# A hybrid decoder layer in fp32 on one core: the last stage's residual rows turned by VectorE, a norm of the first way down by VectorE, three placings

## The chip, the cores and the metric

The kernel runs on one core of one Trainium2 chip. The metric is the device time of one execution in microseconds (us), the median over runs. TensorE is called PE below, its weight loads PEld, VectorE DVE, ScalarE ACT, GpSimd POOL and SyncE SP.

## The reference, cut to what matters

One decoder layer over a sequence of 1024 tokens of width 1024, all in float32:

```
f = swiglu(rmsnorm(h, ffn1_pre_g), ffn1_w_gu, ffn1_w_down);  h = h + 0.5 * rmsnorm(f, ffn1_post_g)
m = hybrid_mixer(rmsnorm(h, mix_pre_g), ...)                  ;  h = h + rmsnorm(m, mix_post_g)
c = memory_cross_attention(rmsnorm(h, xa_pre_g), ...)         ;  h = h + rmsnorm(c, xa_post_g)
f = swiglu(rmsnorm(h, ffn2_pre_g), ffn2_w_gu, ffn2_w_down);  out = h + 0.5 * rmsnorm(f, ffn2_post_g)
swiglu(h) = (silu(g) * u) @ w_down, with g, u the halves of h @ w_gu;  rmsnorm(x, g) = x * rsqrt(mean(x*x) + eps) * g
```

The hidden width of the two feed-forward blocks is 2816. The mixer runs a stick-breaking attention of 16 heads beside a state-space scan (SSD), joins both and multiplies by `w_out`.

## The kernel before, in words

**Precision and tiles.** A float32 number is kept as a high and a low part (`xh`/`xl`, `whi`/`wlo`); a product is three matmuls on PE (`mm3`), each 128x128 by 128x512. ACT makes a high part (CAST, L268, or ACTIVATE, L275), DVE the low part by subtraction (L270, L277). Activations lie with channels on the partitions, in two halves of 512 tokens (half 0 and half 1); the last stage alone has its output with tokens on the partitions.

**Order.** PE's instructions are chained in the order in which the program writes them. A clock of modelled PE time runs along; side work is put on a list with a due time (`self.later`, `at`) and is written when the clock gets there. A scheduler then orders every other engine's instructions, with a priority for what stands in `urgent()`; an engine runs its instructions in the order in which they then stand. `lead` in `turned` is the modelled time by which a norm's matmul is put behind.

**The ways down** (`down7`) multiply by `w_down` with seven block products m = 0 to 6 instead of eight. Each m has eleven pairs of blocks (a weights' block and an activations' block, each split), twelve matmuls a pair, in steps of `sizes` = 2, 1, ..., 2 pairs; m = 6 has 2, 1, 1, 1, 1, 1, 4. In a step, i = 0 to 3 runs over the four banks of PSUM. The last four m's gather in banks `dn`, four buffers, so m + 1 writes the bank that m has left once DVE has added it to `F` (L1141). In the last stage (`down_rows`), bank 3 of m = 6 starts as a copy of `F[1][7]` (ACT, COPY dn<-F, L1152), because `on` is set for i = 3: its matmuls add to the copy. `F[1][7]` is final for that when m = 5's bank 3 has been added and the difference with `F[1][6]` is made. SP loads the blocks to come (`fetch`) into `raw` and `wraw`, two buffers each; for m = 6 DVE adds two blocks of weights into `wc` (L1119) ahead of the split. The activations' split is `hl`.

**The residual of the last stage.** The stored residual `h` has channels on the partitions, the last stage needs tokens there. For half 0, POOL's queue fetches each 128x512 row block by four DMAs of 32x16x32 (`fetch_rows`), and DVE turns it (`turn`, STREAM_TRANSPOSE). For half 1, POOL's queue fetches eight plain 128x512 tiles (`fetch_h`) and PE turns them by eight transposes for each block of 128 tokens (`shift`), between the last matmuls of m = 6; `end` adds the result, read from PSUM, into `F`, and `store` sends it out.

**The first way down** (`down1`) ends with `post(1, ...)`: the norm of the product (`cols`) by four matmuls `ms<-small,bh` into a column and four matmuls `ms<-ident,cpost` into rows, then `apply` (gain, residual) and `low` for each of eight tiles.

**The attention** prepares half of `w_out` beside its own work (`prepare`): load, split, store to DRAM (`dwhi`, `dwlo`), sixteen steps at due times. At its end the output product's operands are split by `mix_split(k)`: k = 0 to 4 by `before(n)` of the last head, 5 to 7 by the product's first two steps.

Of the kernel before, what the change touches and what calls it, by code (L numbers as in the profile page):

```python
# [10 lines left out]
F32 = mybir.dt.float32  # L11
F32R = mybir.dt.float32r
BF16 = mybir.dt.bfloat16
AF = mybir.ActivationFunctionType
ALU = mybir.AluOpType
# [32 lines left out]
class Kern:  # L48
# [296 lines left out]

    def turned(self, accs, ms, wait, c=None, out=None):

        nc, n = self.nc, accs[0].shape[1] // 32
        ps = self.t(self.msp, [P, H], F32, "ms", bufs=1)
        roots = []  # L350
        chains = self.floating is None
        for i, acc in enumerate(accs):
            self.turns += out is None
            part = self.part[self.turns % 2][:, 0:n]
            roots.append(self.roots[self.turns % 4] if out is None else out)
            self.kp(nc.vector.transpose(acc, acc))
            self.kp(
                nc.vector.tensor_reduce(
                    out=part, in_=acc.rearrange("p (j k) -> p j k", k=32), op=ALU.add, axis=mybir.AxisListType.X
                )  # L360
            )
            pin = self.pinned(self.clock + wait) if chains else nullcontext()
            with pin:
                self.mm(ps[:, 16 * i : 16 * i + n], self.one, part, True, True)
        for i, x in enumerate(roots):
            self.kp(nc.scalar.activation(x, ps[:, 16 * i : 16 * i + n], AF.Sqrt, bias=self.eps, scale=ms))
            self.kp(nc.vector.reciprocal(x, x))
        if c is not None:
            for q in range(4):
                k = slice(32 * q, 32 * q + 32)  # L370
                nc.gpsimd.tensor_copy(c[k], roots[0][k].rearrange("p (b q) -> p q b", q=4)[:, q])
        return roots
# [51 lines left out]
    def post(self, hh, gname, r2, gnext=None, out=None, step=None, spread=True, pins=(23000, 28000), accs=None, at=None, tail=None, hold=False, late=None, turn=(False, False), lead=2500):  # L424
# [13 lines left out]
        def cols():  # L438
            if turn[0]:
                roots.extend(self.turned(accs, 1.0 / D_MODEL, lead))  # L440
            else:
                self.rms_cols([accs], c, r2=r2)
# [597 lines left out]
    def down1(self, sp, wdn, act_d, xs_d, gpost, gnext):  # L1040
# [5 lines left out]
        accs = []  # L1046

        def squares(hh, d, tag):
            if d == 0:
# [6 lines left out]
        def finish(m, i):  # L1056
# [5 lines left out]
            elif m == 4:  # L1062
# [4 lines left out]
                self.post(0, gpost, self.C[0], gnext, step=2600, accs=accs[:], tail=(20500, 24000), late=38000, turn=(False, True))  # L1067
            elif m == 5:
                for d in range(4):
                    at(17000 + 2500 * d, squares, 1, d, "bh")  # L1070
# [6 lines left out]
        self.XH[1] = [self.t(self.xp, [P, H], F32R, f"xh1{d}") for d in range(KT)]  # L1077
        self.post(1, gpost, self.C[1], gnext, step=2000, accs=accs[:], at=(6500, 9000, 10000), tail=(7500, 11500), turn=(False, True))

    def down7(self, sp, wdn, act_d, xs_d, place, stay, finish, rows=True):  # L1080

# [60 lines left out]
        for m in range(7):  # L1142
# [13 lines left out]
            for n, size in enumerate(sizes):  # L1156
                ops = take(size)
                for i in range(4):
                    c = slice(i * P, i * P + P)
# [41 lines left out]
    def down_rows(self, sp, wdn, act_d, xs_d, out):  # L1201
# [15 lines left out]

        def fetch_h(d):
            self.kp(nc.gpsimd.dma_start(out=hs[1][d], in_=self.h[1][d]))

        def shift(tb):

            xt = [self.t(self.mmp, [P, H], F32, "mm") for _ in range(2)]
            for d in range(KT):
                self.tr(xt[d // 4][:, (d % 4) * P : (d % 4 + 1) * P], hs[1][d][:, tb * P : (tb + 1) * P])
            return xt

        def fetch_rows(tb, dh, behind):
# [8 lines left out]

        def turn(tb, dh):
            x = hs[0][2 * tb + dh]
            self.kp(nc.vector.transpose(x, x))  # L1240
# [41 lines left out]
        def finish(m, tb):  # L1282
# [11 lines left out]
            elif m == 4:  # L1294
                for tb in range(4):
# [4 lines left out]
                    at(11000 + 12000 * tb, early, tb)  # L1300
                for d in range(KT):
                    at(1000 + 2500 * d, fetch_h, d)
            elif m == 5:
# [14 lines left out]
        def last(tb):  # L1318
            xt = shift(tb)
            for dh in range(2):  # L1320
                end(1, tb, dh, xt)
                store(1, tb, dh, nc.sync)

        self.down7(sp, wdn, act_d, xs_d, place, stay, finish)


# [396 lines left out]
    def attention(self):  # L1723
        nc, ap = self.nc, self.ap
        with self.pools("at", ["o", "a"], ["w"]) as (op, sp, wsp, pp):
            self.prepare([("out", i) for i in range(8, 16)], *self.prep_pool(wsp), [self.clock + 30000 + 20000 * i for i in range(16)])
            turn = [0]
# [142 lines left out]
            def before(n):  # L1870

                for k in range(2 * n, 2 * n + 2) if n < 4 else ():
                    nc.gpsimd.dma_start(out=self.XL[0][k].bitcast(F32), in_=self.mix_d[8 + k][:, 0:H])
                if n > 7:
                    mix_split(n - 8)
                if n == 5:
# [156 lines left out]
            def beside():  # L2033
                mix_row(1)
                self.first = self.mix_first(ready.pop())
                for n in range(4 * MIXED):
                    if n < 2:
                        for k in ((5, 6), (7,))[n]:
                            mix_split(k)
                    if 4 <= n < 11:  # L2040
# [159 lines left out]
    def xattn(self):  # L2200
# [3 lines left out]
        with self.pools("xf", ["a", "b", "w"], []) as (sp, sp2, wsp, pp):  # L2204
# [107 lines left out]
            for s in range(8):  # L2312
# [3 lines left out]
                if s == 4:  # L2316
# [5 lines left out]
                    self.run_later(float("inf"))  # L2322
                    self.post(0, "xa_post_g", None, "ffn2_pre_g", step=5000, at=(5000, 11500, 14500), turn=(True, True))
                if s == 3:
# [245 lines left out]
```

## Time and profile before

| | |
|---|---|
| time, median of 3 runs | 2563.22 us (2559.22 to 2572.07) |
| the profiled execution's own time | 2560.25 us |
| its span on the chip | 2558.5 us |
| PE busy | 2539.2 us, 99% of the span |
| DVE, ACT, POOL busy | 2029.9, 1291.2, 600.2 us |
| instructions | 36552 |

Busy is the time in which an engine works on an instruction; the page gives it for each engine. A timeline row gives the start of a run of like instructions, their time together, and in brackets how long the engine had been idle before it and what released it.

### The profile page before, as it was taken

The page shows a single profiled execution, that of the slowest core. Times are in us where ns is not written, and L with a number is a line of the kernel's source. Part 1 is how long each engine was busy: PE and PEld are TensorE (multiplying, and loading weights), DVE is VectorE, ACT ScalarE, POOL GpSimd, SP SyncE. Part 2 cuts the span into 40 slices and gives each one's busy share as a digit, 9 for nine tenths or more (in the row PEclk, how much of TensorE's full clock was granted, in tenths as well). Part 3 has the DMA queues.
Part 4 walks back from the last instruction along what each step waited for, and adds up shares of the span by engine and source line. Part 5 has one row for each costly group of instructions (what it writes and reads, how often), then busy time and mean ns, then how long its engine had stood idle before and what let it go on. Part 6 is the DMA issues. An engine that isn't in the chain of part 4 may idle for free. (4 is left out here: it accounts for less than half of the span.)

```text
span 2558.5 us, 36552 instructions
## 1 busy us (share of the span) xinstructions
PE 2539.2 (99%) x12570; PEld 2114.6 (83%) x12570; DVE 2029.9 (79%) x3128; ACT 1291.2 (50%) x2305; POOL 600.2 (23%) x726
## 2 busy tenths in 40 slices
PE   9999999999999999999999999999999999999999
PEld 7888888888787778888888898888878888888887
DVE  7988997778789885777877887886767887767777
ACT  7434444555456663555555564455654433334544
POOL 2565554000100001111111110111012655541210
PEclk9999999999999999999999999999999999999999
DMA  6448888664755526666665756647658453326664
GB/s 237 166 176 292 307 293 304 223 199 155 250 195 198 188 75 215 188 180 170 161 174 151 225 151 212 209 158 257 216 182 311 149 160 112 111 79 214 199 187 162
DMA packets 252011, 498.20 MB, mean 195 GB/s; under 512 B 60977, under 2 KB 69553, under 8 KB 251825
## 3 DMA queue, kind: packets, MB, share of 16 engines
q1 hardware_dynamic: 204176, 387.31, 47.0%
q0 software_dynamic: 23744, 65.03, 8.6%
q10 hardware_dynamic: 23904, 43.53, 4.6%
q8 instruction: 99, 1.62, 0.3%
q14 instruction: 88, 0.71, 0.1%
HBM read 331.65 MB, written 143.13 MB: 186 GB/s over the span
## 5 line engine op out<-in xcount | busy, mean ns | idle before, releaser
L139 PE MATMUL mm<-xh,whi 128*128 128x512 f32 x1312 | 515.6, 402 | 3.2 <-ACT xh L275 1.4
L139 PE MATMUL mm<-xh,wlo 128*128 128x512 f32 x1280 | 491.5, 392 | 0.6 <-DMA wlo<-dwlo 0.6
L139 PE MATMUL mm<-xl,whi 128*128 128x512 f32 (+1 forms) x1248 | 485.5, 389 | 1.5 <-DVE xl L277 1.4
L139 PEld LDWEIGHTS mm<-xh,whi 128*128 128x128 f32 x1312 | 246.7, 188 | 45.8 <-issue 4.1
L139 PEld LDWEIGHTS mm<-xh,wlo 128*128 128x128 f32 x1280 | 240.3, 188 | 52.9 <-DMA wlo<-dwlo 1.1
L139 PEld LDWEIGHTS mm<-xl,whi 128*128 128x128 f32 x1248 | 235.2, 188 | 36.6 <-DVE xl L277 3.6
L1910 DVE TENSOR_TENSOR_SCAN nb<-nb,begin 128x128 f32<-128x128 f32 (+7 forms) x128 | 172.0, 1347 | 27.1 <-ACT nb L1906 26.5
L1906 ACT ACTIVATE nb<-z,scale 128x128 f32<-128x128 f32 (+2 forms) x192 | 109.5, 580 | 85.8 <-PE z L139 84.6
L1927 POOL DMA_DIRECT2D mix<-sq x64 | 53.0, 828 | 236.3 <-DVE sq L1925 170.3
L268 ACT CAST whi<-wraw 128x1024 fp32r<-128x1024 f32 (+1 forms) x77 | 73.8, 960 | 67.6 <-PE mm L139 39.4
L270 DVE TENSOR_TENSOR wlo<-wraw,whi 128x1024 fp32r<-128x1024 f32 x61 | 74.3, 1219 | 39.7 <-ACT whi L268 39.6
L730 ACT ACTIVATE ft<-ft 128x512 f32<-128x512 f32 x88 | 55.5, 632 | 95.7 <-DVE ft L729 93.8
L139 PE MATMUL dn<-xh,wlo 128*128 128x512 f32 x296 | 101.0, 389 | 0.0
L833 POOL TENSOR_TENSOR wc<-raw,wraw 128x512 f32<-128x512 f32 x55 | 81.2, 1476 | 56.3 <-DVE blk L270 23.4
L268 ACT CAST ath<-tr 128x512 fp32r<-128x512 f32 (+1 forms) x107 | 58.0, 542 | 68.8 <-PE tr L142 64.1
L833 POOL TENSOR_TENSOR wc<-wraw,raw 128x512 f32<-128x512 f32 x56 | 78.9, 1410 | 53.3 <-DVE whi L270 16.5
L270 DVE TENSOR_TENSOR atl<-tr,ath 128x512 fp32r<-128x512 f32 (+1 forms) x107 | 67.0, 627 | 29.3 <-ACT ath L268 28.5
L932 POOL TENSOR_TENSOR ft<-ft,e 128x512 f32<-128x512 f32 x37 | 59.7, 1613 | 126.3 <-DVE e L928 51.1
L139 PE MATMUL mm<-ath,v 128*128 128x256 f32 x320 | 87.6, 296 | 0.4 <-DVE ev L2010 0.4
L139 PE MATMUL dn<-xh,blk 128*128 128x512 f32 x264 | 85.1, 389 | 0.0
L268 ACT CAST wlo<-wc 128x512 fp32r<-128x512 f32 x79 | 49.1, 621 | 69.2 <-PE dn L139 21.8
L139 PE MATMUL mm<-atl,v 128*128 128x256 f32 x320 | 83.0, 281 | 0.0
(616 smaller groups left out, 6788.5 us busy)
## 6 DMA issues: line engine op xcount, KB each, us to landing
whi<-dwhi SPq DMA_DIRECT2D x82, 512.0 KB, 4.1
wlo<-dwlo SPq DMA_DIRECT2D x82, 512.0 KB, 5.1
wraw<-in_w_gu SPq DMA_DIRECT2D x43, 512.0 KB, 4.1
dwhi<-bh SPq DMA_DIRECT2D x78, 256.0 KB, 4.1
dwlo<-bl SPq DMA_DIRECT2D x78, 256.0 KB, 3.9
raw<-in_w_gu SPq DMA_DIRECT2D x37, 512.0 KB, 4.0
wraw<-xs SPq DMA_DIRECT2D x56, 256.0 KB, 3.1
xs<-ft ACTq DMA_DIRECT2D x54, 256.0 KB, 3.0
```

The lines of the kernel that those rows point to most:

```text
L139: self._pe(self.nc.tensor.matmul(out, lhsT, rhs, start=start, stop=stop, skip_group_check=self.more), cost)
L268: self.kp(self.nc.scalar.copy(hi, src))
L270: self.nc.vector.tensor_tensor(out=lo, in0=src, in1=hi.bitcast(F32), op=ALU.subtract)
L730: nc.scalar.activation(t, t, AF.Silu)
L833: inst = (nc.vector if early else nc.gpsimd).tensor_tensor(out=t, in0=a, in1=b, op=op)
L932: nc.gpsimd.tensor_tensor(out=t1, in0=t1, in1=e, op=ALU.mult)
L1906: nc.scalar.activation(nb[:, s0:s1], z[:, 0:n], AF.Sigmoid, scale=sc[:, i : i + 1])
L1910: nc.vector.tensor_tensor_scan(out=nb[:, 0:Wd][:, ::-1], data0=nb[:, 0:Wd][:, ::-1], data1=begin[:, S - Wd : S][:, ::-1], initial=0.0, op0 ...
L1927: nc.gpsimd.dma_start(out=self.mix_d[p][a * 64 : a * 64 + 64, csl], in_=o, accum_op=ALU.add)
```

## The change

1. In the last stage the half 1 residual is fetched like half 0's: 32 DMAs of 32x16x32 (64 KB each), but on SP's queue, four at a time, each time that `paced(k)` is called: k = 0 to 5 at the steps n = 3 to 8 of m = 4, and k = 6, 7 at n = 0, 1 of m = 5. DVE turns each row block (eight more STREAM_TRANSPOSE). The 32 transposes on PE and POOL's eight fetches go; `end` reads SBUF in place of PSUM.
2. In the first way down, half 1's first norm goes through `turned` (`turn=(True, True)`): DVE transposes and reduces the sum of squares, one matmul `ms<-part,onesr` adds over the partitions, and rows are made by a copy and a transpose. `compact` brings the earlier root into the same form (one transpose, one copy on POOL).
3. All due times of the attention's `prepare` are later by 20000 of the modelled clock.
4. `mix_split(4)` and `(5)` come one call earlier (n = 11, 12), and the two steps at the product's start hold 6 and 7.
5. `post(0)` of the cross attention has `lead=4000` in place of 2500.

```diff
@@ turned
+            y = ps[:, 16 * i : 16 * i + n]
+            if r2 is not None:
+                for y in (y, x):
+                    self.kp(nc.vector.tensor_tensor(out=x, in0=y, in1=r2, op=ALU.mult))
...
@@ down1
+                at(8000, lambda: small.append(self.compact(self.R[1])))
...
-        self.post(1, gpost, self.C[1], gnext, step=2000, accs=accs[:], at=(6500, 9000, 10000), tail=(7500, 11500), turn=(False, True))
+        self.post(1, gpost, small[0], gnext, step=2000, accs=accs[:], at=(6500, 9000, 10000), tail=(7500, 11500), turn=(True, True))
@@ down7
+                k = 9 * (m - 4) + n - 3
+                if paced and 0 <= k < 8:
+                    paced(k)
@@ down_rows
-        def fetch_h(d):
-            self.kp(nc.gpsimd.dma_start(out=hs[1][d], in_=self.h[1][d]))
-        def shift(tb):
-            xt = [self.t(self.mmp, [P, H], F32, "mm") for _ in range(2)]
-            for d in range(KT):
-                self.tr(xt[d // 4][:, (d % 4) * P : (d % 4 + 1) * P], hs[1][d][:, tb * P : (tb + 1) * P])
-            return xt
...
+        def paced(k):
+            rows = self.hall[1].rearrange("(h k) (c e) t -> h e (k c) t", h=2, e=32)[k % 2]
+            x = hs[1][k]
+            for q in range(4):
+                t = k // 2 * P + 32 * q
+                out = x[32 * q : 32 * q + 32, :].rearrange("e (c t) -> e c t", t=32)
+                nc.sync.dma_start(out=out, in_=rows[:, :, t : t + 32])
+            at(3000, turn, k // 2, k % 2, 1)
...
         def last(tb):
-            xt = shift(tb)
             for dh in range(2):
-                end(1, tb, dh, xt)
+                end(1, tb, dh, hs[1][2 * tb : 2 * tb + 2])
@@ attention
-            self.prepare([("out", i) for i in range(8, 16)], *self.prep_pool(wsp), [self.clock + 30000 + 20000 * i for i in range(16)])
+            self.prepare([("out", i) for i in range(8, 16)], *self.prep_pool(wsp), [self.clock + 50000 + 20000 * i for i in range(16)])
...
-                if n > 7:
-                    mix_split(n - 8)
+                for k in {8: (0,), 9: (1,), 10: (2,), 11: (3, 4), 12: (5,)}.get(n, ()):
+                    mix_split(k)
...
-                        for k in ((5, 6), (7,))[n]:
-                            mix_split(k)
+                        mix_split(6 + n)
```

**How the order moves.** DVE in the last stage, where m = 5 ends and m = 6 begins, before. `F<-F,dn` adds a finished bank of m = 5, `F<-F,F` makes the differences (the last of them finishes `F[1][7]`), `wc`, `whi`, `wlo`, `dx` are m = 6's weights, `hl` its activations:

```order
3052 L270 TENSOR_TENSOR whi_24897<-wc_24895,whi_24897 128x512
3053 L270 TENSOR_TENSOR hl_24898<-wraw_24892,hl_24898 128x512
3054 L1141 TENSOR_TENSOR F_4911_23171<-F_4911_23171,dn_24594 128x512
3055 L1119 TENSOR_TENSOR wc_24973<-xh_4925_23185,raw_5260_24970 128x512
3056 L1141 TENSOR_TENSOR F_4913_23173<-F_4913_23173,dn_24595 128x512
3057 L1141 TENSOR_TENSOR F_4912_23172<-F_4912_23172,F_4911_23171 128x512
3058 L1141 TENSOR_TENSOR F_4915_23175<-F_4915_23175,dn_24596 128x512
3059 L1141 TENSOR_TENSOR F_4914_23174<-F_4914_23174,F_4913_23173 128x512
3060 L1141 TENSOR_TENSOR F_4917_23177<-F_4917_23177,dn_24597 128x512
3061 L1251 TENSOR_SCALAR st_24869<-st_24869 128x1
3062 L1141 TENSOR_TENSOR F_4916_23176<-F_4916_23176,F_4915_23175 128x512
3063 L1141 TENSOR_TENSOR F_4918_23178<-F_4918_23178,F_4917_23177 128x512
```

The same place now, from the first `wc` of m = 6 on:

```order
3041 L1136 TENSOR_TENSOR wc_24777<-xh_4932_23190,raw_5215_24774 128x512
3042 L1158 TENSOR_TENSOR F_4910_23168<-F_4910_23168,dn_24621 128x512
3043 L270 TENSOR_TENSOR hl_24780<-raw_5215_24774,hl_24780 128x512
3044 L270 TENSOR_TENSOR wlo_24779<-wc_24777,wlo_24779 128x512
3045 L1158 TENSOR_TENSOR F_4912_23170<-F_4912_23170,dn_24622 128x512
3046 L1280 SCALAR_TENSOR_TENSOR F_4904_23162<-F_4904_23162,rh_5098_24056,xl_4946_23204 128x512
3047 L1158 TENSOR_TENSOR F_4914_23172<-F_4914_23172,dn_24623 128x512
3048 L1136 TENSOR_TENSOR wc_24805<-xh_4933_23191,wraw_24802 128x512
3049 L1158 TENSOR_TENSOR F_4916_23174<-F_4916_23174,dn_24624 128x512
3050 L270 TENSOR_TENSOR hl_24808<-wraw_24802,hl_24808 128x512
3051 L270 TENSOR_TENSOR dx_24807<-wc_24805,dx_24807 128x512
```

And nine rows on, up to that last difference:

```order
3060 L270 TENSOR_TENSOR whi_24857<-wc_24855,whi_24857 128x512
3061 L270 TENSOR_TENSOR hl_24858<-wraw_24852,hl_24858 128x512
3062 L1136 TENSOR_TENSOR wc_24866<-xl_4948_23206,raw_5233_24863 128x512
3063 L270 TENSOR_TENSOR hl_24869<-raw_5233_24863,hl_24869 128x512
3064 L1158 TENSOR_TENSOR F_4911_23169<-F_4911_23169,F_4910_23168 128x512
3065 L270 TENSOR_TENSOR wlo_24868<-wc_24866,wlo_24868 128x512
3066 L1158 TENSOR_TENSOR F_4913_23171<-F_4913_23171,F_4912_23170 128x512
3067 L1271 TENSOR_SCALAR st_24898<-st_24898 128x1
3068 L1158 TENSOR_TENSOR F_4915_23173<-F_4915_23173,F_4914_23172 128x512
3069 L1158 TENSOR_TENSOR F_4917_23175<-F_4917_23175,F_4916_23174 128x512
```

The four adds of m = 5's banks have moved ahead of nearly all of m = 6's weights (ten of its eleven `wc` stand behind the first add now, three did before), and the last difference, nine rows behind the first add before, is 27 rows behind it now.

ACT at the copy that starts m = 6's bank 3, now; `hl_24975` is the activations' block of m = 6's eighth pair, and `sq` a sum of squares:

```order
2376 L268 CAST hl_24927<-wraw_24921 128x512
2377 L268 CAST hl_24938<-raw_5249_24932 128x512
2378 L268 CAST wlo_24868<-wc_24866 128x512
2379 L1268 ACTIVATE st_24911<-st_24911,st_24898 128x1
2380 L268 CAST hl_24975<-wraw_24969 128x512
2381 L1266 ACTIVATE sq_5257_24990,st_24991<-F_4910_23168,cpre_4281_19694 128x512
2382 L1169 COPY dn_24919<-F_4917_23175 128x512
2383 L268 CAST whi_24926<-wc_24924 128x512
```

Before, the copy (`dn_24890`) stands behind the eighth pair's casts too. The buffer `wraw_24969` is the one that `hl_24858` (DVE, row 3061 above) has to have read.

SP in the last stage, now, with the rows' DMAs (L1255) between the loads of the blocks:

```order
1173 L1133 DMA wraw_24435<-act_4304_19737 128x512
1174 L1255 DMA xl_4941_23199<-h_4263_19614 32x16x32 x2
1175 L1122 DMA raw_5168_24462<-in_w_dn 128x512
1176 L1133 DMA raw_5168_24462<-act_4306_19739 128x512
1177 L1255 DMA xl_4941_23199<-h_4263_19614 32x16x32
1178 L1133 DMA wraw_24490<-xs_21010 128x512
1179 L1255 DMA xl_4942_23200<-h_4263_19614 32x16x32 x4
1180 L1133 DMA raw_5175_24516<-xs_21336 128x512
1181 L1255 DMA xl_4943_23201<-h_4263_19614 32x16x32 x4
```

Before, this queue holds the loads alone at this place.

## Rows read from the trace of the kernel before

**Rows 1.** The page: busy time and granted clock.
```profile
PE 2539.2 (99%) x12570; PEld 2114.6 (83%) x12570; DVE 2029.9 (79%) x3128; ACT 1291.2 (50%) x2305; POOL 600.2 (23%) x726
...
PEclk9999999999999999999999999999999999999999
```
**Rows 2.** Timeline of PE and SP in the attention (start, time, what, idle before).
```profile
1041.24 0.42 SPq L224 DMA_DIRECT2D dwlo<-bl  x1
...
1047.82 0.58 SPq L182 DMA_DIRECT2D whi<-dwhi  x1
...
1053.72 0.47 PE L139 MATMUL mm<-xh,whi 128*128 128x512 f32 x1 [1.32 <-DMA whi<-dwhi]
...
1055.05 0.50 PE L139 MATMUL mm<-xh,wlo 128*128 128x512 f32 x1 [0.63 <-DMA wlo<-dwlo]
```
**Rows 3.** Timeline of PE at the output product's start.
```profile
1442.48 0.49 PE L139 MATMUL mm<-xh,whi 128*128 128x512 f32 x1 [0.40 <-ACT xh L275]
1443.52 0.50 PE L139 MATMUL mm<-xl,whi 128*128 128x512 f32 x1 [0.54 <-DVE xl L277]
```
**Rows 4.** Timeline of PE behind the first way down.
```profile
657.18 0.36 PE L139 MATMUL ms<-part,onesr 128*128 128x16 f32 x2
...
663.16 0.40 PE L139 MATMUL mm<-xh,whi 128*128 128x512 f32 x1
663.40 0.95 PE L139 MATMUL ms<-small,bh 128*128 128x1 f32 x8
664.21 0.48 PE L139 MATMUL mm<-xl,whi 128*128 128x512 f32 x1
664.53 0.40 PE L139 MATMUL mm<-xh,wlo 128*128 128x512 f32 x1
...
666.80 1.05 PE L139 MATMUL ms<-ident,cpost 128*128 128x128 f32 x8
```
**Rows 5.** Timeline of PE and DVE at the end of the last stage.
```profile
2544.09 0.60 PE L142 MATMUL mm<-ident,xl 128*128 128x128 f32 x4
...
2544.88 0.94 PE L139 MATMUL dn<-whi,hl 128*128 128x512 f32 x3
...
2553.36 2.04 DVE L1265 SCALAR_TENSOR_TENSOR F<-F,st,mm 128x512 f32<-128x512 f32 x3
```
**Rows 6.** Groups of DVE, last stage, and timeline of POOL: a row block's turn and fetch.
```profile
L1240 DVE STREAM_TRANSPOSE xl<-xl 128x512 f32<-128x512 f32 x4 | 2.8, 704 | 0.0
...
2461.38 2.57 POOL L1236 DMA_DIRECT2D xl<-h  x4
```
**Rows 7.** Timeline of PE: end of m = 5, start of m = 6.
```profile
2513.15 0.84 PE L139 MATMUL dn<-whi,hl 128*128 128x512 f32 x3
...
2517.23 0.84 PE L139 MATMUL dn<-whi,hl 128*128 128x512 f32 x3
2519.34 0.93 PE L139 MATMUL dn<-wlo,hl 128*128 128x512 f32 x3 [1.27 <-DVE F L1141]
...
2523.54 0.96 PE L139 MATMUL dn<-wlo,hl 128*128 128x512 f32 x3
```
**Rows 8.** Timeline of DVE and ACT there.
```profile
2512.92 0.69 DVE L1119 TENSOR_TENSOR wc<-xl,raw 128x512 f32<-128x512 f32 x1 [0.95 <-DMA raw<-in_w_dn]
...
2517.32 0.68 DVE L1141 TENSOR_TENSOR F<-F,dn 128x512 f32<-128x512 f32 x1
2517.92 0.68 DVE L1119 TENSOR_TENSOR wc<-xh,raw 128x512 f32<-128x512 f32 x1
...
2523.99 1.41 DVE L1260 SCALAR_TENSOR_TENSOR F<-F,rh,xl 128x512 f32<-128x512 f32 x2
...
2522.90 0.59 ACT L1152 COPY dn<-F 128x512 f32<-128x512 f32 x1
```
**Rows 9.** Timeline of SP in the last stage, and DMA issues of 2425 to 2520 us.
```profile
2432.11 0.33 SPq L1105 DMA_DIRECT2D raw<-in_w_dn  x1
...
2508.67 0.33 SPq L1105 DMA_DIRECT2D raw<-in_w_dn  x1
...
xl<-h POOLq DMA_DIRECT2D x16, 64.0 KB, 3.6
xl<-h POOLq DMA_DIRECT2D x4, 256.0 KB, 4.2
```
**Rows 10.** Timeline of PE at the program's start.
```profile
1.10 5.27 PE L139 MATMUL ms<-onesr 128*128 128x512 f32 x14 [1.10 <-POOL onesr L2399]
```

More of the change, by code (lines that the diff above doesn't have):

```diff
@@ L344, in rms_cols, with compact, turned @@
             self.kp(nc.vector.tensor_tensor(out=c, in0=c, in1=r2, op=ALU.mult))
-    def turned(self, accs, ms, wait, c=None, out=None):
+    def compact(self, r):
+        self.kp(self.nc.vector.transpose(r, r))
+        self.turns += 1
+        x = self.roots[self.turns % 4]
+        self.kp(self.nc.gpsimd.tensor_copy(x, r.rearrange("p (j k) -> p j k", k=32)[:, :, 0]))
+        return x
+    def turned(self, accs, ms, wait, c=None, out=None, r2=None):
         nc, n = self.nc, accs[0].shape[1] // 32
@@ L365, in turned @@
         for i, x in enumerate(roots):
-            self.kp(nc.scalar.activation(x, ps[:, 16 * i : 16 * i + n], AF.Sqrt, bias=self.eps, scale=ms))
+            y = ps[:, 16 * i : 16 * i + n]
+            if r2 is not None:
+                for y in (y, x):
+                    self.kp(nc.vector.tensor_tensor(out=x, in0=y, in1=r2, op=ALU.mult))
+            self.kp(nc.scalar.activation(x, y, AF.Sqrt, bias=self.eps, scale=ms))
             self.kp(nc.vector.reciprocal(x, x))
+            if r2 is not None:
+                self.kp(nc.vector.tensor_tensor(out=x, in0=x, in1=r2, op=ALU.mult))
         if c is not None:
@@ L439, in cols @@
             if turn[0]:
-                roots.extend(self.turned(accs, 1.0 / D_MODEL, lead))
+                roots.extend(self.turned(accs, 1.0 / D_MODEL, lead, r2=r2))
             else:
@@ L1046, in down1 @@
         accs = []
+        small = []
         def squares(hh, d, tag):
@@ L1077, in down1, with down7 @@
         self.XH[1] = [self.t(self.xp, [P, H], F32R, f"xh1{d}") for d in range(KT)]
-        self.post(1, gpost, self.C[1], gnext, step=2000, accs=accs[:], at=(6500, 9000, 10000), tail=(7500, 11500), turn=(False, True))
-    def down7(self, sp, wdn, act_d, xs_d, place, stay, finish, rows=True):
+        self.post(1, gpost, small[0], gnext, step=2000, accs=accs[:], at=(6500, 9000, 10000), tail=(7500, 11500), turn=(True, True))
+    def down7(self, sp, wdn, act_d, xs_d, place, stay, finish, rows=True, paced=None):
         nc = self.nc
@@ L1236, in fetch_rows, with turn @@
                 self.kp(nc.gpsimd.dma_start(out=out, in_=rows[:, :, t : t + 32]))
-        def turn(tb, dh):
-            x = hs[0][2 * tb + dh]
+        def paced(k):
[6 more added lines that the diff above has]
+            at(3000, turn, k // 2, k % 2, 1)
+        def turn(tb, dh, hh=0):
+            x = hs[hh][2 * tb + dh]
             self.kp(nc.vector.transpose(x, x))
@@ L1300, in finish @@
                     at(11000 + 12000 * tb, early, tb)
-                for d in range(KT):
-                    at(1000 + 2500 * d, fetch_h, d)
             elif m == 5:
@@ L1318, in last @@
         def last(tb):
-            xt = shift(tb)
             for dh in range(2):
-                end(1, tb, dh, xt)
+                end(1, tb, dh, hs[1][2 * tb : 2 * tb + 2])
                 store(1, tb, dh, nc.sync)
-        self.down7(sp, wdn, act_d, xs_d, place, stay, finish)
+        self.down7(sp, wdn, act_d, xs_d, place, stay, finish, paced=paced)
     def ssd(self, close):
@@ L2322, in xattn @@
                     self.run_later(float("inf"))
-                    self.post(0, "xa_post_g", None, "ffn2_pre_g", step=5000, at=(5000, 11500, 14500), turn=(True, True))
+                    self.post(0, "xa_post_g", None, "ffn2_pre_g", step=5000, at=(5000, 11500, 14500), turn=(True, True), lead=4000)
                 if s == 3:
```

## The prediction

> **What bounds the kernel now.** The page comes first: PE is busy for 99% of the span, at the full granted clock (the 2.4 GHz level) in all forty slices [rows 1]. So the time changes by what PE no longer does or newly does, and by what it newly waits or no longer waits; an engine at 79% or 50% matters only where PE waits for it. I then read where PE waits, and what stands on either side of those places in DVE's, ACT's and SP's timelines. Four of PE's waits lie where the diff reaches: for the prepared weights in the attention, 1.32 and 0.63 us [rows 2]; for the split operands where the output product starts, 0.40 and 0.54 us [rows 3]; in the last stage for DVE's add of a finished bank, 1.27 us [rows 7]; and DVE's last additions, which end at 2553.36 + 2.04 = 2555.40 us, behind PE's last transposes [rows 5]. The reader is to see that these are small: all of them come to 0.2% of the span.
>
> A matmul of 128x512 starts 0.227 us after the one before (18 from 2513.15 to 2517.23 [rows 7]), a pair of blocks, twelve matmuls, takes 2.72 us, and m = 4 and 5 together 22 x 2.72 = 59.8 us: m = 4 starts near 2458.1, m = 5 ends near 2517.9.
>
> **The change part by part.** The sum is made against the profiled execution's own 2560.25 us, its span of 2558.5 and 1.75 us around it; that is 2.97 us below the median of the three runs.
>
> *Transposes gone from PE.* Eight take 2544.09 to 2544.88, 0.79 us, and the three matmuls behind them last 0.94 instead of 0.84 [rows 5]: 0.89 us a group. Three of the four groups stand ahead of the last matmul: -2.7 us. The fourth stands between it and DVE's last additions; without it they start one group earlier: -0.9 us.
>
> *Their replacement.* A turn on DVE takes 0.70 us, eight 5.6 us [rows 6], in m = 4 and 5. They stand ahead of m = 5's last splits; DVE has there the time that m = 6's weights took before, which the new order puts later (next part), so I price them at 0. Four row DMAs take 2.57 us of a queue's issue time [rows 6]: 32 come to 20.6 us on SP. SP loaded m = 4's first block at 2432.11 [rows 9], 26 us before its use; that lead covers them: 0. Without it, up to 20.6 us.
>
> The rows' transfers are the place where a rule speaks against the change. Half 0's 64 KB pieces land after 3.6 us, the plain 256 KB tiles after 4.2 us [rows 9]: per byte 3.4 times as slow, but never longer than a tile, so I keep 0. By the Trainium skill, DMA: Bandwidth & Descriptors, Specifications, a piece below 512 B falls short of line rate, since it is read, modified and written; these have runs of 128 B. The rows agree per byte; by the rule alone the loads beside them would be late, which is rival 3.
>
> *DVE's order at the end of m = 5.* This is the term that decides. DVE is to run the first add of a bank of m = 5 right behind the first `wc` of m = 6. That bank is complete at 2513.15 + 0.84 = 2514.0 [rows 7]. Before, DVE did other work there, came to this add at 2517.32 [rows 8], and PE waited 1.27 us for it. Now the add is in time and that wait goes. But what DVE did ahead of the add now stands behind it, and between it and the difference that finishes `F[1][7]`. From the add to that difference are 28 rows: 22 of 0.60 us (2517.32 to 2517.92), four with a scalar of 0.70 (1.41 for two), two small ones of 0.15 [rows 8]: 16.3 us, so the difference is ready at 2530.3, and the copy into bank 3 (0.59 us [rows 8]) at 2530.9. Before, the copy started at 2522.90 and PE's first matmul of bank 3 at 2523.54, right behind it [rows 7, 8]: just in time.
>
> There is a second path to the copy. On ACT it stands behind the cast of m = 6's eighth activations' block. That block's buffer comes free with the 20th row from the first add: 15 x 0.60 + 4 x 0.70 + 0.15 = 12 us, at 2526.0. A load took 4.25 us from its issue at 2508.67 to the DVE instruction that waited for it at 2512.92 [rows 8, 9]: 2530.3; then the cast, a square and the copy, three at about 0.6: 2532.1. PE comes to bank 3 some 1.36 us a bank after 2517.9, delayed by about 1.5 us at the second pair, whose weights DVE finishes ten rows behind the first add, at 2520.2: so at 2523.5, as before. It then stands still until 2530.9 to 2532.1, 7.4 to 8.6 us. I take the later path: **+8.6 us**. The old wait of 1.27 us is in that: both executions reach bank 3 at the same moment. Behind it nothing more is late: DVE has 57 rows from the first add to the last weights (40 x 0.60 + 11 x 0.70 + 6 x 0.15 = 32.6 us, 2546.6), and PE wants them two us into its last step, which begins at 2532.1 + 1.4 + 5 x 2.72 = 2547.1.
>
> *PE after standing still.* The longest of the waits above is 1.32 us, so no row shows PE coming back from eight. The nearest is its start: 14 matmuls of this shape last 5.27 us [rows 10] instead of 13 x 0.227 + 0.39 = 3.34. Between 0 and this 1.9 us I take 1.9, as standing still is what the two have in common. The granted clock there reads full [rows 1], so the rows do not tell why. The Trainium skill, TensorE: Matmul & The Clock Gate, Part 1 (The HAM clock gate), says that an idle PE falls to 1.2 GHz and has to work some time before it gets 2.4 GHz again; by it the return from 8.6 us is slow too. No run here shows it so far.
>
> *First way down.* From 663.16 to 664.21 lie 1.05 us where matmuls without the eight `bh` records stand 0.23 apart, and the next comes 0.32 later: 0.91 us go. The eight `cpost` records behave alike (1.05 us busy): another 0.9. The new `part` matmul gives back 0.3 (0.36 busy) [rows 4]: -1.5 us. DVE's two further transposes and a reduction, about 0.7 us each by a turn's [rows 6], and the copy between make half 1's tiles about 2.5 us later; PE has half 0's products to do meanwhile, so I price them at 0. If that cover failed, it would cost those 2.5 us.
>
> *Attention's prepared weights.* One step, a load and two stores of 0.42 us each, goes from SP's queue between 1040 and 1042 (the last issue at 1041.24), ahead of the load at 1047.82 for which PE waits at 1053.72 [rows 2]. Three issues are 1.2 us, the waits together 1.95; nothing, if SP waits for something else between. I take -1.2, bounds 0 and 1.95.
>
> *Splits of the output product.* The split that PE waits for comes a call earlier, and both waits [rows 3] go with about 0.1 us of restart each: -1.1, bound 0. `lead` moves one short matmul behind six others where PE does not wait: 0.
>
> Sum: 8.6 + 1.9 - 2.7 - 0.9 - 1.5 - 1.2 - 1.1 = +3.1 us; 2560.25 + 3.1 = 2563.4 us. No change by what a measurement of this kernel can tell (0.5%, 12.8 us).
>
> **Rivals.**
> 1. *DVE's order does no harm* (PE reaches the place later, or the adds come when the splits are done). Then the wait at the start of m = 6 goes, 1.4 us with its restart, and all gains stay: -2.7 - 0.9 - 1.4 - 1.5 - 1.2 - 1.1 = -8.8: 2551.4. For it: DVE reaches the add early, since ten of the splits before it have moved. Against it: what moved is exactly what then stands between the add and the copy, and DVE's order is fixed.
> 2. *The stall comes, the slow return does not*: 2561.5. For it: PE's clock is full in every slice.
> 3. *The rows' fetches starve m = 5*: the side of slower. Between m = 5's loads stand four fetches, 2.57 us, and a load of 0.33 and its partner, over 2.9 us, where a pair lasts 2.72. If SP has no lead there (its buffers are four, and freed only when split), each of eight groups shows, up to 20.6 us; it decides from the point at which over 7 us of these are uncovered, and with 10 the time is 2573. Against it: 26 us of lead at 2432.
> 4. *PE's waits in the attention stay, and new ones take the place at the output product*: both placings give 0, 2565.7.
>
> **How the numbers follow.** The forecast, with the slow return, 0.4; rival 2, 0.22; rival 1, 0.2; rival 3, 0.1; rival 4, 0.08. The range goes from rival 1's 2551.4, a little raised because the median lies above this execution, to 2570: the forecast with 0 for the three gains elsewhere (2567.2) and the median's 2.97 on top. That leaves a part of rival 1 and most of rival 3 out: 2552 to 2570. Faster by over 0.5% would need less than 2550.4: the edge of rival 1, 0.05. Slower needs more than 2576: rival 3 with over 12 us uncovered, 0.04. Within: 0.91.
>
> **What would show it.** In the profile after: a wait of PE of 7 to 9 us near 2523 (counted in this stage's own time) for ACT's copy into `dn`, the difference `F<-F,F` at 16 us behind the first `F<-F,dn`, and matmuls wider apart than 0.227 us behind it; no transposes in the last stage; no PE wait for `dwhi` near 1053 and none at 1442 to 1444; 1.5 us less of PE near 663 to 668. The prediction is wrong if PE comes to bank 3 with the copy done (rival 1), or waits for `whi`, `wlo` or `hl` in m = 5 (rival 3).

## The result, and the profile after

The changed kernel takes 2569.02 us (median of 22 runs, 2566.71 to 2573.21), the kernel before 2564.05 us in 22 runs beside it (2559.22 to 2572.07): ratio 1.0019, 95% interval 1.0013 to 1.0024. It is slower by 5 us (0.19%): clear of the noise, and less than the 0.5% from which the prediction counts a change. Its profiled execution took 2567.96 us, 7.7 more than that of before; its span is 2566.2 us.

The page, busy time and granted clock, to be held against [rows 1]:

```profile
PE 2537.2 (99%) x12524; PEld 2112.3 (82%) x12524; DVE 2038.8 (79%) x3140; ACT 1295.7 (50%) x2305; POOL 596.7 (23%) x719
...
PEclk9999999999999999999999999999999999999998
```

PE works 2 us less and the span is 7.7 us longer: the time went into waiting, and for the first time a slice of the clock is not full. Where, the timeline of PE in the last stage shows (start, time, what, idle before and its releaser):

```profile
2517.37 0.84 PE L139 MATMUL dn<-wlo,hl 128*128 128x512 f32 x3
2518.65 0.50 PE L139 MATMUL dn<-dx,hl 128*128 128x512 f32 x1 [0.44 <-ACT dx L268]
2519.80 0.72 PE L139 MATMUL dn<-dx,hl 128*128 128x512 f32 x2 [0.65 <-DVE dx L270]
...
2522.44 0.84 PE L139 MATMUL dn<-dx,hl 128*128 128x512 f32 x3
2530.82 1.65 PE L139 MATMUL dn<-wlo,hl 128*128 128x512 f32 x3 [7.54 <-ACT dn L1169]
2532.27 5.45 PE L139 MATMUL dn<-dx,hl 128*128 128x512 f32 x15
2537.56 2.88 PE L139 MATMUL dn<-whi,hl 128*128 128x512 f32 x12
```

m = 6 starts without the old wait of 1.27 us [rows 7], waits 1.1 us at the second pair, and then stands 7.54 us for ACT's copy into bank 3. Behind it three matmuls last 1.65 us where three lasted 0.84, and eighteen take 2530.82 to 2537.56, 6.74 us in place of 18 x 0.227 = 4.09. The same stretch by windows (busy time of PE, PEld, DVE, ACT and POOL, granted clock, DMA share, GB/s):

```profile
2488.00:2518.00 30.00, 30.00 (x134) 24.69 (x132) 19.70 (x35) 13.89 (x29) 1.16 (x2) 1.00 0.50 150
2518.00:2540.00 22.00, 13.37 (x45) 10.12 (x45) 22.00 (x40) 12.89 (x27) 2.16 (x4) 0.77 0.54 179
```

The clock was full until the wait and falls behind it, and DVE, busy 19.70 of 30 us before, has no free moment after. Its timeline shows the turn:

```profile
2506.31 0.69 DVE L1136 TENSOR_TENSOR wc<-xh,raw 128x512 f32<-128x512 f32 x1
2513.49 0.69 DVE L1158 TENSOR_TENSOR F<-F,dn 128x512 f32<-128x512 f32 x1 [6.49 <-PE dn L139]
...
2528.39 1.29 DVE L1158 TENSOR_TENSOR F<-F,F 128x512 f32<-128x512 f32 x2
```

And ACT's what stands ahead of the copy:

```profile
2528.57 0.30 ACT L1268 ACTIVATE st<-st,st 128x1 f32<-128x1 f32 x1 [1.91 <-DVE st L1271]
2528.95 0.62 ACT L268 CAST hl<-wraw 128x512 fp32r<-128x512 f32 x1
2529.47 0.72 ACT L1266 ACTIVATE sq<-F,cpre 128x512 f32<-128x512 f32 x1
2530.10 0.19 ACT L1266 ACTIVATION_READ_ACCUMULATOR sq<-F,cpre 128x1 f32 x1
2530.19 0.58 ACT L1169 COPY dn<-F 128x512 f32<-128x512 f32 x1
```

DVE idles 6.49 us for m = 5's first bank and then needs 16.2 us from the first add to the end of the last difference (2529.68). The copy starts 0.5 us later, behind the eighth pair's cast and the square on ACT.

The rest of the program can be read from landmarks, starts of the same matmul in both timelines:

| PE at | before | after | lead so far |
|---|---|---|---|
| first way down, m = 1's first matmuls | 472.93 | 473.62 | +0.69 |
| state-space scan | 746.43 | 746.41 | -0.02 |
| behind it, `mm<-xs,wlo` | 985.92 | 986.22 | +0.30 |
| attention, behind the prepared weights | 1055.05 | 1053.89 | -1.16 |
| behind the output product's start | 1511.37 | 1510.49 | -0.88 |
| cross attention, `ms<-part` | 1886.16 | 1885.37 | -0.79 |
| m = 6's first matmul (before: without its wait) | 2517.91 | 2517.37 | -0.54 |
| m = 6's bank 3 | 2523.54 | 2530.82 | +7.28 |
| the last six matmuls | 2549.96 | 2557.96 | +8.00 |
| end of the span | 2558.5 | 2566.2 | +7.70 |

So all but the last stage gave 0.5 us, and the last stage, from m = 6's first matmul to the end, went from 40.6 to 48.8 us. That stretch is the measure for the experiments below, since the parts ahead of it differ by some us from one profiled execution to the next. Waits of PE outside the last stage, after, where the predicted gains lay ([rows 2, 3]):

```profile
473.62 5.74 PE L139 MATMUL dn<-hl,dx 128*128 128x512 f32 x24 [1.51 <-ACT F L1197]
...
1053.89 0.50 PE L139 MATMUL mm<-xh,wlo 128*128 128x512 f32 x1 [0.75 <-DMA wlo<-dwlo]
...
1444.07 0.50 PE L139 MATMUL mm<-xl,whi 128*128 128x512 f32 x1 [1.46 <-DVE xl L277]
1445.31 0.50 PE L139 MATMUL mm<-xl,whi 128*128 128x512 f32 x1 [0.28 <-DVE xl L277]
```

### The profile page after: what moved, and what is told of

Read it like the earlier page. It is cut to its first block, busy times and chain, and to the rows that moved or that the text cites. A ratio compares the mean times of both kernels' runs of the same rounds, so it can differ in the third digit from the quotient of the medians.

```text
span 2566.2 us, 36484 instructions
## 1 busy us (share of the span) xinstructions
PE 2537.2 (99%) x12524; PEld 2112.3 (82%) x12524; DVE 2038.8 (79%) x3140; ACT 1295.7 (50%) x2305; POOL 596.7 (23%) x719
## 5 line engine op out<-in xcount | busy, mean ns | idle before, releaser
L139 PE MATMUL dn<-xh,whi 128*128 128x512 f32 x240 | 82.7, 389 | 0.0
```

The source lines that it names most:

```text
L139: self._pe(self.nc.tensor.matmul(out, lhsT, rhs, start=start, stop=stop, skip_group_check=self.more), cost)
```

## The experiments

Each is timed beside the kernel before on the same chip; `stage` is the stretch from m = 6's first matmul (without a wait ahead of it) to the span's end, from the trace. It comes from one execution of each run, and a kernel whose last stage is that of before (rest_only) has 44.4 us for 40.6: a difference of less than some 4 us between two stages needs the medians beside it.

| run | stage, us | median, us | ratio to before, 95% |
|---|---|---|---|
| before | 40.6 | 2564.05 | 1 |
| the change | 48.8 | 2569.02 | 1.0019 (1.0013 to 1.0024) |
| last_only | 48.6 | 2571.77 | 1.0027 (1.0017 to 1.0036) |
| rest_only | 44.4 | 2562.56 | 0.9991 (0.9982 to 1.0000) |
| no_copy | 47.5 | 2569.08 | 1.0018 (1.0009 to 1.0027) |
| plain_add | 44.4 | 2566.07 | 1.0007 (0.9999 to 1.0016) |
| fill | 46.6 | 2568.93 | 1.0014 (1.0004 to 1.0023) |
| banks | 41.7 | 2563.80 | 0.9993 (0.9984 to 1.0002) |
| banks_pool | 44.2 | 2566.33 | 1.0003 (0.9994 to 1.0012) |
| act_rows | 47.7 | 2568.22 | 1.0014 (1.0004 to 1.0023) |
| pool_rows | 36.8 | 2558.80 | 0.9978 (0.9968 to 0.9987) |
| pool_last | 36.8 | 2559.47 | 0.9976 (0.9965 to 0.9987) |
| best | 36.8 | 2556.89 | 0.9969 (0.9959 to 0.9979) |

**Which part loses: last_only, rest_only.** The kernel before with part 1 alone (`paced`, the turns, no transposes), and with parts 2 to 5 alone.

> Part 1 alone (the last stage's rows) on the kernel before. Theory A (the copy into bank 3 comes late because DVE's adds of m = 5 moved ahead of m = 6's weights, and PE's clock falls behind the wait): the whole loss lies here, a PE wait of 7 to 8 us for ACT's copy near 2523 us, a granted clock below 1 behind it, and 5 to 7 us more than the kernel before (the other parts gave PE a lead of only 0.5 us at the end of m = 5 in the changed kernel's trace). Theory B (the loss is spread: the other parts' new waits and the rows' fetches): at most 2 us more than before.

> Parts 2 to 5 without part 1, on the kernel before. Theory A: 0.5 to 1.5 us less than the kernel before, as PE's lead at the end of m = 5 was 0.5 us; no wait for a copy in the last stage but the old 1.3 us for the add. Theory B: 2 to 5 us more than before. The prediction's own terms for these parts were -3.8 us together.

Part 1 alone shows the same wait; row of PE's timeline:

```profile
2538.87 1.65 PE L139 MATMUL dn<-wlo,hl 128*128 128x512 f32 x3 [7.99 <-ACT dn L1152]
```

It costs 6.6 us by the medians (2571.77 to 2565.15), in the range expected by theory A, and theory B's at most 2 falls. The other parts gave 2.6 us, more than theory A's 0.5 to 1.5 and less than the prediction's 3.8; the interval, from no change to 4.6 us, allows both. The run with them alone had a surprise in the last stage, whose code and DVE order are those of before:

```profile
2522.71 0.94 PE L139 MATMUL dn<-wlo,hl 128*128 128x512 f32 x3 [3.61 <-DVE F L1158]
...
2524.38 1.48 PE L139 MATMUL dn<-wlo,hl 128*128 128x512 f32 x3
```

The wait for the first add, 1.27 us in [rows 7], was 3.61 us here (DVE had waited 3.34 and 2.54 us for loads), and behind it groups of three matmuls start up to 1.28 us apart, in place of 0.68. The profiled execution of before was a good one: the median of its 22 runs lies 3.8 us above it.

**Whether the copy is the cause: no_copy.** Bank 3 is gathered like the others.

```diff
-                inside = rows and m == 6
+                inside = False
```

> The changed kernel with bank 3 of m = 6 gathered like the other three (no copy at its start, DVE adds the bank to F at its end). Theory A: the wait of 7.5 us and the slow clock behind it go, but DVE still stood idle 6.5 us for m = 5's first bank, so PE comes to its last step at about 2538 and waits there some 5 us for the last pair's weights (in the changed kernel's trace they are ready at 2545.4); in all 3 to 7 us less than the changed kernel. Theory C (once the copy is out of the way nothing is late): 10 us less. Theory B: no change within 1 us.

The wait for the copy went, and the time stayed (1.0018 for 1.0019); theory A's 3 to 7 us less was wrong. PE now waits where the splits come late, at its last step:

```profile
2545.61 0.50 PE L139 MATMUL dn<-dx,hl 128*128 128x512 f32 x1 [1.47 <-ACT dx L268]
2546.89 2.05 PE L139 MATMUL dn<-dx,hl 128*128 128x512 f32 x3 [0.78 <-DVE dx L270]
2549.36 1.22 PE L139 MATMUL dn<-dx,hl 128*128 128x512 f32 x2 [0.42 <-DVE dx L270]
...
2554.69 0.84 PE L139 MATMUL dn<-whi,hl 128*128 128x512 f32 x3
```

The three rows hold 2.7 us of waits, where some 5 were expected, and matmuls are slow again behind them (three in 2.05 us). From 2541.97 to 2554.69 PE ran 24 matmuls, 12.72 us for 24 x 0.227 = 5.44: the 7.3 us lost here are about what the copy had cost. The copy is where DVE's lateness shows; without it the lateness shows 20 us later.

**DVE's order: plain_add.** m = 5's adds are written without the priority, so that on DVE five `wc` and their splits go ahead of the first.

```diff
-                    with self.urgent():
+                    with nullcontext() if rows and m == 5 else self.urgent():
```

> The changed kernel with m = 5's four adds written without the priority, so that on DVE the first stands 18 rows later, behind five wc and their splits. Theory A: DVE works through what it idled for (6.5 us), PE waits 0.5 to 1 us at the start of m = 6 and 1 to 2 us for the copy, the clock stays full: 6 to 9 us less than the changed kernel, 1 to 4 less than before. Theory B: no change within 1 us.

3 us less than the change, not 6 to 9: the wait for the copy is gone, but DVE comes late to the adds themselves:

```profile
2528.53 1.62 PE L139 MATMUL dn<-wlo,hl 128*128 128x512 f32 x3 [5.00 <-DVE F L1158]
```

**The slow return: fill.** 34 matmuls into a spare bank ahead of bank 3's first; their result is not used.

```diff
+                    if inside and n == 0 and i == 3:
+                        spare, now, self.inlater = self.t(self.mmp, [P, H], F32, "mm"), self.clock, True
+                        for z in range(34):
+                            self.mm(spare, ops[0][0][:, 0, c], ops[0][1][:, 0], True, True)
+                        self.clock, self.inlater = now, False
```

> The changed kernel with 34 matmuls more, of no use to the output, ahead of bank 3's first one in m = 6: they go to a spare bank and fill the wait of 7.5 us with work. Theory A (the clock falls because PE stands still): the wait is gone or under 1 us, the granted clock stays full from 2518 to 2540, the matmuls behind it are 0.227 us apart at once, and the time is 2 to 3 us below the changed kernel's. Rival (the matmuls behind the wait are slow for another reason, their operands or banks): still slow behind it, no change within 1 us.

```profile
2525.40 7.87 PE L139 MATMUL mm<-hl,wlo 128*128 128x512 f32 x34
2533.44 0.96 PE L139 MATMUL dn<-wlo,hl 128*128 128x512 f32 x3 [0.17 <-ACT dn L1169]
2534.24 3.57 PE L139 MATMUL dn<-dx,hl 128*128 128x512 f32 x15
```

PE works through the wait, and the matmuls behind it are fast at once (15 in 3.57 us for 5.45); the granted clock from 2518 to 2540 was 1.00 where it had been 0.77. The slow matmuls follow from standing still. So the expectation for the trace came true and its rival fell. The time is another matter: the stage is 2.2 us shorter, by the ratios (1.0014 and 1.0019) it is 1.3 us, less than the 2 to 3 expected, and the intervals don't tell that from nothing.

**More room for DVE: banks, banks_pool.** m = 6 in PSUM buffers that the transposes have left, without the copy, with plain adds; then also m = 6's sums of weights on POOL.

```diff
-                    self.t(self.mmp, [P, H], F32, "mm") if m == 4 and i < 3 else ...
+                    self.t(self.mmp, [P, H], F32, "mm") if (m == 4 or rows and m == 6) and i < 3 else ...
```

> The changed kernel with m = 5's adds without the priority, no copy, and m = 6's banks 0 to 2 in the PSUM buffers that the transposes have left, so that PE waits for no add where m = 6 starts. Theory A widened (DVE as a whole is late from m = 5 on; the copy is where it shows): no wait at the start of m = 6, but 2 to 5 us of waits at its last step for the last pairs' weights; 3 to 5 us less than the changed kernel. Theory C (only the adds and the copy are in the way): 10 us less.

> As the run with the spare banks, and m = 6's eleven sums of two blocks of weights by POOL in place of DVE (6.6 us less of DVE, about 16 us more of POOL at some 1.45 us each by its like additions elsewhere). Theory A widened: PE's waits in m = 6 fall below 2 us, 8 to 11 us less than the changed kernel and 3 to 6 less than before. Theory D (ACT's casts and the loads hold m = 6 as much as DVE): 4 us less than the changed kernel at most.

(In the kernel before, m = 4 too gathers three of its four banks in the transposes' buffers, as the edit shows; only m = 5 and m = 6 have all four of theirs in `dn`.) The first did what theory A widened expected in kind: no wait at m = 6's start, 2 us of them at its last step.

```profile
2544.76 0.73 PE L139 MATMUL mm<-dx,hl 128*128 128x512 f32 x2 [0.78 <-DVE dx L270]
2546.01 0.50 PE L139 MATMUL mm<-dx,hl 128*128 128x512 f32 x1 [0.52 <-ACT dx L268]
2547.23 0.73 PE L139 MATMUL mm<-dx,hl 128*128 128x512 f32 x2 [0.71 <-DVE dx L270]
```

It gave 6.7 us against the change by the ratios to before (0.0026 of 2564), more than the 3 to 5 expected. All row fetches are still on SP's queue here, and the time is that of before: fetches on SP's queue do not by themselves make the loss.

The second missed its 8 to 11 us: it is 4.1 us below the change by the ratios, and 2.5 us above `banks` by the medians, which the intervals don't tell from nothing. PE stood 2.13 us for an add and again at the last step. The timelines of POOL, DVE and PE there:

```profile
2515.80 1.73 POOL L1136 TENSOR_TENSOR wc<-xh,raw 128x512 f32<-128x512 f32 x1
2517.49 1.74 POOL L1136 TENSOR_TENSOR wc<-xh,wraw 128x512 f32<-128x512 f32 x1
```

```profile
2516.30 1.77 DVE L270 TENSOR_TENSOR hl<-wraw,hl 128x512 fp32r<-128x512 f32 x1
2518.00 1.78 DVE L270 TENSOR_TENSOR dx<-wc,dx 128x512 fp32r<-128x512 f32 x1
```

```profile
2529.79 0.96 PE L139 MATMUL dn<-wlo,hl 128*128 128x512 f32 x3 [2.13 <-DVE F L1158]
```

Most of DVE's instructions beside an addition on POOL took 1.7 us in place of 0.69, so that DVE was busy 2045.2 us in all, with eleven additions fewer, for 2039.4 in `banks`. The run therefore does not show what less work on DVE is worth, and says nothing for or against theory D, which was not followed further.

**The queue: pool_rows, act_rows.** The row fetches on POOL's queue, and on ACT's.

```diff
-                nc.sync.dma_start(out=out, in_=rows[:, :, t : t + 32])
+                nc.gpsimd.dma_start(out=out, in_=rows[:, :, t : t + 32])
```

> The changed kernel with the 32 row fetches on POOL's queue in place of SP's. Theory A: no change within 1.5 us, the wait of 7 to 8 us for the copy stays. Rival 3 of the prediction (the fetches on SP's queue make the loads and the last stage late): 3 us less or more, and the wait shrinks.

> The changed kernel with the row fetches on ACT's queue. SP's queue then holds loads alone, and yet DVE's order stays near the changed kernel's (one wc ahead of m = 5's adds, five more behind them before the last difference). Theory A (the order alone makes the loss): PE again waits over 5 us for the copy or the adds, and the time is within 2 us of the changed kernel's. Theory E (the fetches hold SP's queue, loads and splits come late, and the order only follows): the loss goes as with the fetches on POOL, 6 to 10 us less than the changed kernel, and no wait of PE over 2 us in m = 6.

On POOL's queue the loss is gone and a gain is there, 10 us below the change, against theory A as it was written down, and as rival 3 would have it; act_rows and `banks` are what tells the two apart. But the queue also changes DVE's order. There six `wc` of m = 6 stand ahead of the first add, and DVE runs through them without a gap; DVE's and PE's timelines:

```profile
2518.95 0.68 DVE L1158 TENSOR_TENSOR F<-F,dn 128x512 f32<-128x512 f32 x1
```

```profile
2522.33 0.84 PE L139 MATMUL dn<-wlo,hl 128*128 128x512 f32 x3
...
2526.41 0.84 PE L139 MATMUL dn<-wlo,hl 128*128 128x512 f32 x3
```

m = 6 begins at 2522.33 and comes to bank 3 at 2526.41, 4.08 us later, six matmuls a bank at full speed, no wait. On ACT's queue SP's is as free as on POOL's, but DVE's order stays near the changed one, and nearly the whole loss stays (47.7 us of stage for 48.8, 1.3 us less by the ratios):

```profile
2530.14 1.65 PE L139 MATMUL dn<-wlo,hl 128*128 128x512 f32 x3 [7.98 <-ACT dn L1169]
```

DVE idles there for m = 5's first bank as in the changed kernel, 5.18 us for 6.49:

```profile
2513.19 0.69 DVE L1158 TENSOR_TENSOR F<-F,dn 128x512 f32<-128x512 f32 x1 [5.18 <-PE dn L139]
```

So a free SP queue does not bring the time back, which speaks against rival 3 and theory E, as `banks` does from the other side; the loss goes with DVE's order. One doubt is that on ACT's queue the fetches take ACT's own issue time, and ACT makes the copy. The trace leaves little of it: ACT issued the last of them at 2497.36, DVE's last difference ended at 2528.56, and the copy started at 2529.51, so at most 0.95 us of the 7.98 is ACT's own delay.

What the queue does is to move DVE's order. With SP's fetches and m = 5's adds written without the priority (plain_add) the stage is still 7.6 us longer than with POOL's, so the order further ahead matters too. It shows in the 30 us up to m = 6's first matmul; the runs are before, pool_rows, plain_add, act_rows (columns as above):

```profile
2487.91:2517.91 30.00, 30.00 (x134) 24.64 (x132) 26.41 (x47) 18.60 (x38) 3.24 (x6) 1.00 0.68 220
```

```profile
2492.33:2522.33 30.00, 30.00 (x135) 24.82 (x133) 29.99 (x54) 18.90 (x38) 2.22 (x4) 1.00 0.69 220
```

```profile
2493.36:2523.36 30.00, 30.00 (x134) 24.63 (x132) 23.90 (x42) 18.01 (x38) 1.16 (x3) 1.00 0.59 185
```

```profile
2487.07:2517.07 30.00, 30.00 (x135) 24.82 (x133) 22.03 (x39) 13.91 (x29) 1.16 (x2) 1.00 0.56 158
```

DVE was busy 29.99 us with POOL's fetches, 26.41 before, 23.90 in plain_add, 22.03 in act_rows and 19.70 in the change, and the stages, 36.8, 40.6, 44.4, 47.7 and 48.8 us, stand in the same order: in these five executions the stage is the longer the more DVE idles ahead of m = 6, which fits the cause and does not prove it. In plain_add DVE's waits in these 30 us are for ACT's casts (1.03, 0.83, 1.93 and 1.97 us the longest), which pool_rows has not. DVE's waits for loads follow no such order: 3.45 us in three waits before, 1.51 us in act_rows, none in the other three. Why the scheduler places the splits otherwise when the fetches are POOL's, no trace shows; that is left open.

**Part 1 alone, and the best: pool_last, best.** The fetches on POOL's queue: with part 1 alone; and with parts 1 to 3.

> Part 1 alone, with the row fetches on POOL's queue, on the kernel before. If part 1's own gain is the transposes and the tail, as the prediction's terms had it (2.7 + 0.9, and 1.4 for the wait at the start of m = 6): 3 to 6 us less than before, stretch from the end of m = 5 to the span's end near 37 us. If the gain of the run with the fetches on POOL came from parts 2 to 5: within 1.5 us of before.

> Parts 1 (fetches on POOL), 2 and 3, with the output product's splits and the lead as before. By the landmarks between the waits part 4 cost 0.3 us and not gained 1.1: so 0 to 2 us less than with all parts and the fetches on POOL, 7 to 9 us less than before. If part 4 is worth its predicted 1.1 us: 1 us more than with all parts.

Part 1 by itself is worth 6.0 us (2559.47 to 2565.44) when DVE's order is good. `best` leaves the output product's splits and the lead as before; it is the fastest, 8.6 us below the kernel before timed beside it. Against pool_rows it is 2.3 us by the ratios (0.0009), more than expected, and the intervals don't tell it from nothing; so what the output product's splits are worth is read from landmarks, below. Its waits at the output product are those of before, 0.40 and 0.53 us:

```profile
1440.95 0.51 PE L139 MATMUL mm<-xh,whi 128*128 128x512 f32 x1 [0.40 <-ACT xh L275]
1441.98 0.50 PE L139 MATMUL mm<-xl,whi 128*128 128x512 f32 x1 [0.53 <-DVE xl L277]
```

## Why the prediction was right, point by point

The forecast, a small loss in which the last stage eats the other gains, came true: 2569.02 us in the range of 2552 to 2570, near its upper end, for 2563.4. Of the 5.6 us between, 3.8 are the base: the sum was made against a profiled execution that lies 3.8 us below the median of 22 runs. The rest is size: the sum said +3.1, the medians differ by +5.0, the two traces by +7.7. The mechanism was right, the gains elsewhere were not. The terms of the last stage come to +6.9, and its stretch grew by 8.2; those outside it come to -3.8, and the traces give -0.5 (the medians of rest_only up to -2.6). The range held because its upper end had been worked out for that case, with nothing for the gains elsewhere.

- **DVE's order, +8.6: right in place and kind, 7.8 measured.** The first add came at 2513.49, in time, the last difference 16.2 us later (16.3 worked out), the copy started 0.5 us behind it, the eighth cast and a square ahead of it on ACT. So it went by the first path, 7.4 us, and the sum had taken the second, 8.6. In that path the eighth block's load took 4.25 us; here its cast started 3.1 us after its issue (2525.84 to 2528.95). Bank 3 came 13.45 us after m = 6's first matmul for 5.63 before: 7.82. The order as the cause rests on pool_rows (another order, no wait, stage 36.8 us) beside act_rows (SP's queue as free, the order nearly the changed one, 47.7), and on `banks` (SP's queue as full, time of before); that the copy alone is not the cause, no_copy showed. The remark that nothing is late behind it held: no wait of PE at the last step.
- **The slow return, +1.9: 2.65 measured** over the eighteen matmuls against full speed, 2.5 against the eighteen of before (2523.54 to 2527.77, 4.23 us): more than the upper bound of 1.9, which the program's start had given. Fill showed it to follow from standing still, so rival 2 falls. The granted clock, full until the wait, reads 0.77 over the stretch with it, between the levels of 1.2 and 2.4 GHz, and the matmuls run at half speed and then at full. The Trainium skill, TensorE: Matmul & The Clock Gate, Part 1 (The HAM clock gate), says that an idle PE falls to the lower level and has to work before it gets the upper one again; the traces of the change and of fill agree with it.
- **The transposes and the tail, -2.7 and -0.9: too much.** Only two of the four groups stand ahead of the last six matmuls (2549.96 before), not three; from bank 3 to those six, 26.42 before and 27.14 after, the slow return's 2.5 less the transposes: -1.8, two groups of 0.89. Behind them to the span's end 8.54 and 8.24 us: -0.3. With the 7.82 above the stage's +8.2 is whole. The error was to count the third group as PE's, when DVE's additions beside it set the end.
- **First way down, -1.5: -0.7** between 473 and 746, and +0.7 ahead of it, where PE waits for an ACT copy of a bank (0.67 before, 1.51 after, 0.67 to 2.46 over all runs, with and without part 2). So this wait is the execution's, not the change's. The matmuls that went were sized right: the same matmul starts at 647.87 us before and at 649.23 after, 1.36 later, and at 746 nothing of that is left, so PE gains 1.4 us. Ahead of them, at 646 to 649, new and longer waits take 0.7 back, so that by these landmarks part 2 is worth about 0.7 us. The prediction had priced the cover for the later tiles at 0.
- **Attention, -1.2: -1.46 by the landmarks; right in size, in part by luck.** The wait for `whi` went, 0.75 us for `wlo` stay: 1.95 us of waits before, 0.75 after, and 0.69 to 0.91 in the runs with part 3 for 1.83 to 2.07 in those without. But SP issued the load only 0.34 us earlier (1047.48), since it now waits for something else between (at 1040.56 to 1043.76), which the prediction had named as the case worth nothing. The wait went because the load landed 4.0 us after its issue for 5.8 before; why, no trace shows.
- **Output product, -1.1: failed, 0.0.** The two waits and a third of 0.28 us (1446.62) became one of 1.46 and one of 0.28. From the matmuls ahead of it (1437.01 before, 1435.69 after) to the last of these waits' PE needed 9.61 us before and 9.62 after; best and pool_last, without part 4, have 9.61. The split that PE waited for came earlier, and PE then waited for the next `xl` of DVE's: the step "both waits go" looked at the releaser of each wait and not at what DVE still had to do behind it. The 0.28 us that the table loses by 1511 are not part 4's: they come from a later wait (0.80 us for 0.39), which best has without part 4 (0.77) and rest_only with it has not (0.39). The 0.3 in best's expectation is that.
- **Rival 1** (full gain) is what pool_rows and pool_last show with another queue; 2551.4 was its price against the profiled execution, 36.8 us of stage for 40.6. **Rival 3** has no sign in the changed kernel's PE rows (no long wait for `whi`, `wlo` or `hl` in m = 5), and act_rows and `banks` speak against it. **Rival 4** came half true: at the output product a new wait took the place of the old, in the attention most of the waits went.

## What to carry to other kernels

An in-order engine with idle time pays for an instruction that is placed early: the add that was in time made DVE stand 6.5 us and put everything behind it late, so look in the new order for what stands *behind* a moved wait, and count to the next instruction that another engine needs. Which queue issues a transfer can reorder another engine entirely where a scheduler plans them together; try the same change on each queue before giving it up (here 1.0019 became 0.9978). And a single profiled execution is no base for a sum of a few us: compare a stretch between two landmarks, in several traces.

## What was not expected of the hardware

Shorter waits than the 8 us of the prediction slowed PE too. Behind the 3.61 us of rest_only the next groups of three matmuls started 0.89, 1.28, 1.28 and 0.88 us apart, where 0.68 is three times 0.227. Near 474 us the granted clock over 460 to 480 us was 0.91 in the four traces whose wait there was 2.04 to 2.46 us (no_copy, last_only, pool_rows, plain_add), and 1.00 with waits of 0.67 (before), 1.43 (best), 1.51 (after) and 1.79 (banks). The 24 matmuls behind that wait took 7.17 to 7.35 us in those four and 5.74 in these. The row of pool_rows (columns as above):

```profile
460.00:480.00 20.00, 17.57 (x72) 14.09 (x71) 18.39 (x32) 12.93 (x24) 0.00 (x0) 0.91 0.58 193
```

So a wait can cost more than its length in one execution and only its length in another. That may be a part of the spread of these kernels' runs (2559 to 2572 us for the kernel before); no run tested it.

DVE slowed beside POOL: in banks_pool most of its instructions of 128x512 took 1.7 us while POOL made an addition of the same size, and 0.69 us without one. What two engines share there, no run shows.
